# Three PSUM banks for the attention's logits instead of two, one for the output projection instead of two

## The chip, the cores and the metric

The kernel runs on one core of one Trainium2 chip. The metric is the device time of one execution in microseconds (us). TensorE is called PE in the profile, its weight loads PEld; VectorE is DVE, ScalarE is ACT, GpSimd is POOL, SyncE (which here only issues DMAs) is SP. PSUM is the small memory that PE writes its results to; it has 8 banks, each 128 partitions by 512 float32.

## What is computed

One layer of a decoder trunk, 1024 tokens by 1024 channels, float32. The reference, cut to what matters here:

```python
h = rms_norm(x, norm_mix_pre)
q, k_c, v_c, k_s, v_s, k_w, v_w, gate, u, v = split(h @ w_in)
# 8 heads, 3 branches each, on blocks of 128 queries:
p_c = softmax(q @ kc.T + bias)          # compressed keys (63)
p_s = softmax(q @ k_s.T + bias)         # selected blocks (here all of the causal ones)
p_w = softmax(q @ k_w.T + bias)         # window of 512
nsa = g0 * p_c @ vc + g1 * p_s @ v_s + g2 * p_w @ v_w
gm  = gelu(u) * (w_s @ layer_norm(gelu(v)) + b_s)
h1  = x + rms_norm(concat(nsa, gm) @ w_out, norm_mix_post)
out = h1 + rms_norm(swiglu(rms_norm(h1, norm_ffn_pre)), norm_ffn_post)
```

## The kernel before

The work is cut into tiles of 128 tokens, and runs in this order.

1. **Input side (0 to some 265 us).** `norm_in` normalizes and transposes the tokens; `vu_half` multiplies them by the v and u columns of `w_in` (into banks `ps_a` and `ps_w`); `spatial`, `proj_t`, `compress_in`, `compress_out` and `v_proj` make the gating part (kept in DRAM as `gm_scr`), the queries (in DRAM as `q_scr`), keys (`kt`) and values (`vt`). Every product that must be exact to float32 is made of three matmuls of split operands (`mm3`, L183 to L185).
2. **Attention (some 244 to 592 us).** The loop at L640 takes the tiles 7, 6, ... 0, and in each tile four pairs of heads. For a head, `logits` (L671) makes one chunk of logits of up to 512 columns in a bank `ps_a`, by two matmuls (L674, L675); DVE takes it out of the bank with the bias added, or plain (`biased` L679, `plain` L683), into the row buffer `L`. ACT makes the exponentials (L722), POOL multiplies by the gate over the sum (L733), PE transposes (L745, banks `ps_t`), ACT and DVE split the result (`ph`, `pl`, L167 and L173), and PE multiplies by the values (L752, L754, bank `ps_p`). `otmp`, `os`, `mixh`, `mixl` (L756 to L761) are the pair's result.
3. **Output projection.** While the attention of a tile runs, `output_proj` (L596) multiplies the result of the tile before by `w_out`: two halves `nh` of 512 columns, 24 matmuls each, of which 12 read the gating part `gmh` and 12 the attention's `mixh`, `mixl`. Each half has a bank `ps_w`; ACT reads the bank twice (L614 square, L615 copy). Then come the norm (L617 to L622), a store of `h1`, and `pre_ffn` (L626): square, scale (L628, L630), eight transposes (L634, banks `ps_t`), a scaling on DVE (L636) and a store to `h2_scr`.
4. **FFN (from some 597 us).** First `plain_pass` (L881) over tokens 512 to 1023 in banks `ps_a`, `ps_w`, `ps_p`, from operands `b12`, `b22` (profile name `b_b12t`, `b_b`) and `plain_op`; then these pools are closed, and the eight banks become the ring `fb`, in which all the rest is done. The second `plain_pass` needs the tokens 0 to 511, so the `h2` of tile 0.

The lines that matter for the change:

```python
109  TAGS = {"a": 2, "t": 3, "p": 1, "w": 2}
118  def bank(tag):
119      return psp[tag][1].tile([P, 512], F32, name="ps_" + tag)
121  for tag in ("a", "w", "t", "p"):
122      psp[tag] = pool("ps_" + tag, TAGS[tag], space=PSUM)
340  ps = turn("proj", "aaaw")
484  ps = turn("vproj", "wpt")
591  PVB, OPB, OB = "p", "w", 1
607  for nh in range(2):
608      ps = turn("opj", OPB)
610      for k in range(KD):
613          mm3(ps, sh, sl, wo[kk][0][:, cs], wo[kk][1][:, cs], k == 0, k == KD - 1)
614      nc.scalar.activation(h1[:, cs], ps, AF.Square, accum_out=s2[:, nh:nh + 1])
615      nc.scalar.copy(h1[:, cs], ps)
672  ps = bank("a")
674  nc.tensor.matmul(ps[:, :w], qt[:, 0, hh, :], kt_[g][:, c0:c0 + w], start=True, stop=False)
675  nc.tensor.matmul(ps[:, :w], qt[:, 1, hh, :], kt_[g][:, c0:c0 + w], start=False, stop=True)
776  return turn("plain", "awap")
```

`turn` (L113) takes the pools of a string in turn: L340 is in `proj_t`, L484 in `v_proj`, L776 in the first `plain_pass`; L607 to L615 are `output_proj`, L672 to L675 `logits`. A tile of a pool with n buffers waits until the tile n places before it in the same pool has been read. The order of the instructions on each engine is not the order of the code: the framework puts them in order when the kernel is built, by a plan of when each could run (`schedule_with_timeline_sim=True`, L1210) and by the priorities in the code (`tc.high_priority(...)`, L648 to L735). On the chip every engine then runs its own list strictly in order, and waits at the first instruction that is not ready.

Of the kernel before, what the change touches and what calls it, by code (L numbers as in the profile page):

```python
# [70 lines left out]
def trunk_kernel(ctx, tc, x, rel_bias, norm_mix_pre, norm_mix_post, norm_ffn_pre, norm_ffn_post, w_in,  # L71
# [7 lines left out]
    def pool(name, bufs, side=None, **kw):  # L79
        if side is not None:  # L80
            kw["side"] = side
        g = tc.tile_pool(name=name, bufs=bufs, reuse_waits="tile", **kw)
        return g, g.__enter__()
# [22 lines left out]
    psp = {}  # L106
    dram = ctx.enter_context(tc.tile_pool(name="dram", bufs=1, space=DRAM))

    TAGS = {"a": 2, "t": 3, "p": 1, "w": 2}

    turns = {}

# [8 lines left out]
    for tag in ("a", "w", "t", "p"):  # L121
        psp[tag] = pool("ps_" + tag, TAGS[tag], space=PSUM)
    for tag in ("whi", "wlo"):
# [1090 lines left out]
```

## Time and profile before

| | |
|---|---|
| median of 3 runs | 1249.96 us (1245.37 to 1250.56) |
| the profiled execution, its own time | 1250.03 us |
| its span, first to last instruction | 1248.3 us |
| PE busy | 1201.0 us, 96% of the span |
| DVE busy | 922.4 us, 74% |
| ACT busy | 568.4 us, 46% |
| POOL busy | 383.4 us, 31% |
| mean granted TensorE clock | 0.993 |

Busy time of PE is the union of its matmuls from start to modelled end; as matmuls overlap, a busy PE can still have started fewer of them than it could. The count of instructions in a stretch (the x in the windows) tells more. "Idle before" is the time that an engine stood still just ahead of an instruction, and the name behind the arrow is what ended it. An "until" list of a line gives the same for all instructions of that line, with total time and count.

### The profile page before, as it was taken

What the parts mean: (1) busy time and instruction counts of PE and PEld (TensorE: products, weight loads), DVE (VectorE), ACT (ScalarE), POOL (GpSimd) and SP (SyncE); (2) the same over time, 40 slices, a digit from 0 to 9 for tenths busy, and PEclk for the clock granted to TensorE, in tenths of its full rate; (3) what the DMA queues carried; (4) which work ended last, traced back from release to release, by engine and by line L of the source; (5) the groups of instructions that cost most, each with busy time, mean ns of one, the idle gap of its engine ahead of it and who ended that gap; (6) DMA issues with size and microseconds to landing.
All of it is one profiled execution on the core that took longest, in us unless ns stands there. A gap on an engine that the chain in (4) does not pass through costs nothing.

```text
span 1248.3 us, 18189 instructions
## 1 busy us (share of the span) xinstructions
PE 1201.0 (96%) x6074; PEld 1008.8 (81%) x6074; DVE 922.4 (74%) x2071; ACT 568.4 (46%) x1254; POOL 383.4 (31%) x454
## 2 busy tenths in 40 slices
PE   6999999889999999998899999999999999999997
PEld 5888878878888888887687888888888888888886
DVE  5646237668898988986599887876787647588996
ACT  4423022246777878886544332333332324444452
POOL 3315113155445446562051222201222101132341
PEclk9999999999999999999999999999999999999999
DMA  7212453321021121424414233223233189332235
GB/s 259 86 66 87 135 178 117 106 93 48 10 81 43 48 81 48 140 77 137 145 65 152 100 120 127 94 89 108 91 127 124 53 287 359 122 110 85 94 119 202
DMA packets 106229, 143.86 MB, mean 115 GB/s; under 512 B 8120, under 2 KB 64792, under 8 KB 106136
## 3 DMA queue, kind: packets, MB, share of 16 engines
q1 hardware_dynamic: 99552, 133.43, 32.4%
q0 software_dynamic: 2304, 4.20, 1.2%
q10 hardware_dynamic: 4280, 5.08, 1.2%
q8 instruction: 48, 0.79, 0.3%
q14 instruction: 45, 0.37, 0.1%
HBM read 103.60 MB, written 40.71 MB: 116 GB/s over the span
## 4 chain that ended last, share of the span: by engine, by line
PE 84%; DVE 9%; ACT 2%; issue 2%; DMA 1%; POOL 1%; SPq 0%; DVEq 0%; POOLq 0%; ACTq 0%
PE fb L185 16%; PE fb L183 15%; PE fb L184 15%; PE ps_w L183 4%; PE ps_w L184 4%; PE ps_w L185 4%; PE ps_a L183 4%; PE ps_a L184 3%; PE ps_a L185 3%; PE ps_t L745 3%; PE ps_p L754 2%; PE ps_p L752 2%; PE ps_a L674 2%; PE ps_a L675 2%; DVE pl L173 1%
## 5 line engine op out<-in xcount | busy, mean ns | idle before, releaser
L967 DVE TENSOR_TENSOR cc<-fb,cc 128x512 f32<-128x512 f32 x140 | 94.2, 685 | 55.9 <-PE fb L185 55.1
L722 ACT ACTIVATE L<-L,mm 128x64 f32<-128x64 f32 (+8 forms) x192 | 116.2, 608 | 37.0 <-DVE mm L679 36.2
L733 POOL TENSOR_SCALAR L<-L,wts 128x64 f32<-128x64 f32 (+8 forms) x192 | 108.4, 588 | 74.1 <-DVE wts L728 53.4
L848 POOL TENSOR_TENSOR cc<-sil 128x512 f32<-128x512 f32 x22 | 35.2, 1601 | 287.4 <-issue 226.3
L173 DVE TENSOR_TENSOR pl<-ps_t,ph 128x512 fp32r<-128x512 f32 (+1 forms) x160 | 101.6, 643 | 11.2 <-ACT ph L167 10.6
L167 ACT CAST op<-s 128x512 fp32r<-128x512 f32 x80 | 49.4, 620 | 121.5 <-PE fb L185 106.7
L184 PE MATMUL fb<-wdo,hido 128*128 128x512 f32 x264 | 102.7, 389 | 0.0
L183 PE MATMUL fb<-wdo,hido 128*128 128x512 f32 x264 | 101.9, 389 | 0.0
L185 PE MATMUL fb<-wdo,hido 128*128 128x512 f32 x264 | 100.4, 389 | 0.0
L184 PE MATMUL fb<-b_b,op 128*128 128x512 f32 x256 | 99.6, 389 | 0.0
L183 PE MATMUL fb<-b_b,op 128*128 128x512 f32 x256 | 99.3, 389 | 0.0
L185 PE MATMUL fb<-b_b,op 128*128 128x512 f32 x256 | 99.3, 389 | 0.0
L167 ACT CAST ph<-ps_t 128x512 fp32r<-128x512 f32 (+1 forms) x160 | 84.4, 555 | 25.6 <-PE ps_t L745 23.1
L745 PE MATMUL ps_t<-ident,L 128*128 128x128 f32 x592 | 88.6, 274 | 1.5 <-DVE pl L173 0.9
L674 PE MATMUL ps_a<-kt,qt 128*128 128x448 f32 (+4 forms) x208 | 74.7, 363 | 7.3 <-DVE L L683 2.8
L173 DVE TENSOR_TENSOR hido<-hidr,hido 128x512 fp32r<-128x512 f32 x77 | 60.8, 801 | 27.3 <-ACT hido L167 27.2
L167 ACT CAST hido<-hidr 128x512 fp32r<-128x512 f32 x77 | 47.4, 619 | 66.3 <-PE fb L185 22.8
L1046 POOL TENSOR_TENSOR tt<-wdr 128x512 f32<-128x512 f32 x22 | 36.1, 1644 | 134.5 <-DVE wdo L173 80.1
L754 PE MATMUL ps_p<-pl,vt 128*128 128x256 f32 x264 | 74.3, 303 | 3.1 <-DVE pl L173 3.0
L745 PEld LDWEIGHTS ps_t<-ident,L 128*128 128x128 f32 x592 | 68.9, 141 | 9.5 <-POOL L L733 1.8
L167 ACT CAST op<-wraw 128x512 fp32r<-128x512 f32 x60 | 37.1, 622 | 84.3 <-PE fb L185 75.6
L173 DVE TENSOR_TENSOR op<-s,op 128x512 fp32r<-128x512 f32 x80 | 63.9, 804 | 14.6 <-ACT op L167 13.8
(359 smaller groups left out, 3468.2 us busy)
## 6 DMA issues: line engine op xcount, KB each, us to landing
wraw<-in_w_gate_up_dram SPq DMA_DIRECT2D x40, 512.0 KB, 3.6
hidr<-hid_scr SPq DMA_DIRECT2D x77, 256.0 KB, 2.7
hid_scr<-sil SPq DMA_DIRECT2D x44, 256.0 KB, 2.0
wdr<-in_w_down_dram SPq DMA_DIRECT2D x44, 256.0 KB, 5.5
hid_scr<-cc SPq DMA_DIRECT2D x33, 256.0 KB, 2.0
xt<-in_x_dram SPq DMA_DIRECT2D x16, 512.0 KB, 3.6
raw<-in_w_in_dram SPq DMA_DIRECT2D x16, 512.0 KB, 4.3
gm_scr<-gmt SPq DMA_DIRECT2D x16, 256.0 KB, 2.6
```

The lines of the kernel that those rows point to most:

```text
L167: nc.scalar.copy(hi, src)
L173: e.tensor_tensor(lo, src, fl(hi), op=ALU.subtract)
L183: nc.tensor.matmul(ps, sh, mh, start=first, stop=False)
L184: nc.tensor.matmul(ps, sh, ml, start=False, stop=False)
L185: nc.tensor.matmul(ps, sl, mh, start=False, stop=last)
L674: nc.tensor.matmul(ps[:, :w], qt[:, 0, hh, :], kt_[g][:, c0:c0 + w], start=True, stop=False)
L722: nc.scalar.activation(L[:, c0:c1], L[:, c0:c1], AF.Exp, bias=mm[:, col:col + 1], scale=-1.0, accum_out=sums[:, hh, br:br + 1])
L733: nc.gpsimd.tensor_scalar(pts[hh][:, c0:c1], pts[hh][:, c0:c1], wts[:, hh, br:br + 1], 1.0, op0=ALU.mult, op1=ALU.mult)
L745: nc.tensor.transpose(ps[:, (bi * 2 + hh) * P:(bi * 2 + hh + 1) * P], pts[hh][:, c0:c0 + P], ident)
L754: nc.tensor.matmul(pv[:, :256], v, pl[:, bi * 256:(bi + 1) * 256], start=False, stop=last)
L967: nc.vector.tensor_tensor(dst, ps, y_, op=ALU.add)
L1046: eng.tensor_tensor(dst, x_, y_, op=op)
```

## The change

```diff
-    TAGS = {"a": 2, "t": 3, "p": 1, "w": 2}
+    TAGS = {"a": 3, "t": 3, "p": 1, "w": 1}
```

The pool of `ps_a` gets a third bank, and that of `ps_w` keeps one; the sum stays eight. Nothing else is edited. No instruction is added or removed, but since the plan sees other waits, the order on the engines changes in many places. Three of them follow. The names with numbers are the program's tiles; a number is the same tile in both versions.

PE, early in the attention, around the chunk of logits `ps_a_2879` of tile 7. Before:

```order
L754 MATMUL ps_p_2563<-pl_2648,vt_1425 128x256
L674 MATMUL ps_a_2865<-kt1_1419,qt_2483 128x256
L675 MATMUL ps_a_2865<-kt1_1419,qt_2483 128x256
L674 MATMUL ps_a_2874<-kt1_1419,qt_2483 128x448
L675 MATMUL ps_a_2874<-kt1_1419,qt_2483 128x448
L674 MATMUL ps_a_2879<-kt1_1419,qt_2483 128x384
L675 MATMUL ps_a_2879<-kt1_1419,qt_2483 128x384
L674 MATMUL ps_a_2883<-kt1_1419,qt_2483 128x256
L675 MATMUL ps_a_2883<-kt1_1419,qt_2483 128x256
L745 MATMUL ps_t_2779<-ident_123,L_2675 128x128
```

Now:

```order
L745 MATMUL ps_t_2616<-ident_123,L_2526 128x128
L674 MATMUL ps_a_2879<-kt1_1419,qt_2483 128x384
L675 MATMUL ps_a_2879<-kt1_1419,qt_2483 128x384
L674 MATMUL ps_a_2883<-kt1_1419,qt_2483 128x256
L675 MATMUL ps_a_2883<-kt1_1419,qt_2483 128x256
L754 MATMUL ps_p_2563<-pl_2596,vt_1425 128x256
L752 MATMUL ps_p_2563<-ph_2595,vt_1425 128x256
```

The same chunk stands 53 rows earlier in PE's list (row 1394 before, 1341 now), ahead of value products (`ps_p_2563`) that it used to follow. Over most of the attention 5 to 11 more of the 208 chunks have been issued after about the same number of PE's matmuls, and 14 to 32 fewer of the output projection's 384; at the end of the attention both are level again.

PE, the change from the output projection of tile 1 (second half: `ps_w_6795`) to that of tile 0 (first half: `ps_w_7076`). Before:

```order
L754 MATMUL ps_p_6878<-pl_6885,vt_1425 128x256
L752 MATMUL ps_p_6878<-ph_6895,vt_1425 128x256
L754 MATMUL ps_p_6878<-pl_6896,vt_1425 128x256
L183 MATMUL ps_w_7076<-whi_2055,gmh_7069 128x512
L184 MATMUL ps_w_7076<-wlo_2056,gmh_7069 128x512
```

Now:

```order
L752 MATMUL ps_p_6947<-ph_6964,vt_1425 128x256
L754 MATMUL ps_p_6947<-pl_6965,vt_1425 128x256
L185 MATMUL ps_w_6795<-whi_2670,mixl_6236 128x512
L183 MATMUL ps_w_7076<-whi_2055,gmh_7069 128x512
L184 MATMUL ps_w_7076<-wlo_2056,gmh_7069 128x512
```

`ps_w_6795` and `ps_w_7076` are now one and the same bank, and the last matmul of the one stands right ahead of the first of the other. Before, the two halves of a tile were open at the same time and taken in turn; now the second half begins when the first is done.

PE, behind the last value products of the attention (`ps_p_7039`, tile 0). Before:

```order
L754 MATMUL ps_p_7039<-pl_7057,vt_1425 128x256
L183 MATMUL ps_w_7076<-whi_2670,mixh_6684 128x512
L184 MATMUL ps_w_7076<-wlo_2671,mixh_6684 128x512
L183 MATMUL ps_w_7103<-whi_2670,mixh_6684 128x512
L184 MATMUL ps_w_7103<-wlo_2671,mixh_6684 128x512
L185 MATMUL ps_w_7076<-whi_2670,mixl_6685 128x512
L185 MATMUL ps_w_7103<-whi_2670,mixl_6685 128x512
L183 MATMUL ps_a_7310<-b_b12t3_7261,plain_op_7264 128x512
```

Now:

```order
L754 MATMUL ps_p_7039<-pl_7057,vt_1425 128x256
L183 MATMUL ps_w_7076<-whi_2670,mixh_6684 128x512
L184 MATMUL ps_w_7076<-wlo_2671,mixh_6684 128x512
L185 MATMUL ps_w_7076<-whi_2670,mixl_6685 128x512
L183 MATMUL ps_a_7310<-b_b12t3_7261,plain_op_7264 128x512
L184 MATMUL ps_a_7310<-b_b12t3_7261,plain_op_7264 128x512
L183 MATMUL ps_w_7103<-whi_2055,gmh_7069 128x512
L184 MATMUL ps_w_7103<-wlo_2056,gmh_7069 128x512
```

The second half of tile 0 (`ps_w_7103`, 24 matmuls) used to be nearly done here; now it begins here, behind two matmuls of the FFN's first pass.

## Rows read from the trace of the kernel before

**Rows 1.** The page: busy time by engine, and the chain that ended last.
```profile
PE 1201.0 (96%) x6074; PEld 1008.8 (81%) x6074; DVE 922.4 (74%) x2071; ACT 568.4 (46%) x1254; POOL 383.4 (31%) x454
PE 84%; DVE 9%; ACT 2%; issue 2%; DMA 1%; POOL 1%; SPq 0%; DVEq 0%; POOLq 0%; ACTq 0%
```

**Rows 2.** Windows: stretch and length, busy (and count) by engine, clock, DMA share, GB/s.
```profile
100.00:200.00 100.00, 100.00 (x480) 83.08 (x479) 49.76 (x82) 17.93 (x35) 30.58 (x25) 1.00 0.41 128
200.00:300.00 100.00, 91.49 (x560) 79.71 (x558) 67.39 (x208) 43.42 (x94) 38.64 (x47) 0.97 0.33 103
300.00:400.00 100.00, 97.05 (x631) 85.03 (x630) 86.84 (x329) 73.45 (x178) 44.30 (x70) 1.00 0.15 43
400.00:500.00 100.00, 96.02 (x639) 84.99 (x637) 87.55 (x348) 78.57 (x207) 50.04 (x85) 1.00 0.18 55
560.00:620.00 60.00, 52.71 (x268) 43.45 (x267) 38.21 (x108) 36.06 (x89) 11.19 (x25) 0.94 0.43 138
700.00:1248.00 548.00, 540.13 (x2383) 447.05 (x2382) 410.66 (x586) 197.91 (x353) 115.07 (x78) 1.00 0.40 134
```

**Rows 3.** Line 674, first matmul of a logits chunk: what ended its idle time.
```profile
  PE ps_a L675: 6.7, 11
  DVE mm L679: 4.2, 12
  DVE L L683: 3.8, 11
```

**Rows 4.** Line 679, DVE taking logits out: what ended its idle time.
```profile
  PE ps_a L675: 24.6, 29
```

**Rows 5.** Timeline of PE, tile 1's projection to tile 0's (start, length, engine, line).
```profile
576.28 0.72 PE L185 MATMUL ps_w<-whi,mixl 128*128 128x512 f32 x2
579.12 0.50 PE L183 MATMUL ps_w<-whi,gmh 128*128 128x512 f32 x1 [1.19 <-ACT h L615]
```

**Rows 6.** Timeline of ACT, the same stretch.
```profile
577.04 0.61 ACT L614 ACTIVATE h<-ps_w 128x512 f32<-128x512 f32 x1
577.63 0.60 ACT L614 ACTIVATE h<-ps_w 128x512 f32<-128x512 f32 x1
578.45 0.62 ACT L615 COPY h<-ps_w 128x512 f32<-128x512 f32 x1
```

**Rows 7.** Timeline of all engines, from that projection to tile 1's transposes.
```profile
584.47 0.39 PE L185 MATMUL ps_w<-whi,gmh 128*128 128x512 f32 x1
584.70 0.28 PE L752 MATMUL ps_p<-ph,vch 128*128 128x256 f32 x1
584.76 1.15 ACT L630 ACTIVATE xt<-h,rstd 128x1024 f32<-128x1024 f32 x1 [0.85 <-POOL rstd L179]
585.41 0.40 PE L183 MATMUL ps_w<-whi,gmh 128*128 128x512 f32 x1
588.16 1.04 PE L634 MATMUL ps_t<-ident,xt 128*128 128x128 f32 x8
589.04 0.60 PE L745 MATMUL ps_t<-ident,L 128*128 128x128 f32 x4
591.35 0.38 PE L754 MATMUL ps_p<-pl,vch 128*128 128x256 f32 x1
```

**Rows 8.** Timeline of all engines, end of the attention to the FFN's first matmul.
```profile
592.75 0.37 ACT L756 COPY otmp<-ps_p 64x256 f32<-64x256 f32 x1 [0.56 <-PE ps_p L754]
593.02 2.18 ACT L167 CAST b_b12t<-b_r1t 128x512 fp32r<-128x512 f32 x4
594.65 0.50 PE L183 MATMUL ps_w<-whi,mixh 128*128 128x512 f32 x1 [1.99 <-DVE mixh L169]
595.11 2.18 ACT L167 CAST b_b<-b_r1t 128x512 fp32r<-128x512 f32 x4
597.18 0.62 ACT L167 CAST plain_op<-plain_raw 128x512 fp32r<-128x512 f32 x1
597.86 0.50 PE L183 MATMUL ps_a<-b_b12t,plain_op 128*128 128x512 f32 x1 [1.55 <-ACT plain_op L167]
```

**Rows 9.** Timeline of all engines, tile 0's transposes to the FFN's second half.
```profile
616.59 1.03 PE L634 MATMUL ps_t<-ident,xt 128*128 128x128 f32 x8
617.22 1.29 DVE L636 TENSOR_TENSOR h2s<-ps_t,gffn 128x512 f32<-128x512 f32 x2 [1.72 <-PE ps_t L634]
624.01 2.38 ACT L167 CAST b_b<-raw 128x512 fp32r<-128x512 f32 x4 [5.52 <-DMA raw<-h_scr]
```

**Rows 10.** DMA issues of `gmh`: size of one, median us from issue to landing.
```profile
gmh<-gm_scr POOLq DMA_DIRECT2D x16, 256.0 KB, 3.7
```

## The prediction

> **What bounds the kernel now.** I read the page first: PE is busy 96% of the span, and 84% of the chain that ended last is PE [rows 1]. So the time is PE's work plus what PE stands still, and the change has no other way to pay than through PE's waits. The windows by stage tell where those are [rows 2]. From 100 to 200 us PE is busy all the time; from 700 us on it starts 2383 matmuls in 548 us, nearly all of 512 columns, which is one every 0.23 us. Nothing can be gained there. From 200 to 620 us PE is not full, and beside it DVE is busy 87% to 88% and ACT 73% to 79% of the attention's middle: three engines that hand work to each other, with little room in any.
>
> Then I looked at what the two pools of the change make PE wait for. PE's first matmul of a logits chunk (L674) found its engine idle until DVE had taken out an earlier chunk: 4.2 us in 12 cases and 3.8 us in 11, and 6.7 us more in 11 cases are put down to PE's own matmul before [rows 3]. In turn DVE, taking logits out at L679, waited 24.6 us in 29 cases for PE [rows 4]. That is the picture of two engines that share two banks: each waits for the other by turns. For `ps_w` the trace shows one clear wait: ahead of tile 0's projection PE stood 1.19 us for ACT's reading of a bank [rows 5].
>
> **The change part by part.** The profiled execution took 1250.03 us, 0.07 above the median of the runs shown, so I sum against 1250.03.
>
> *Input side: 0.* `vu_half` uses `ps_w` once in every 48 matmuls; 24 of `ps_a` (5.4 us at 0.23) lie between, and cover one ACT reading of about 0.6 us, the length of L614 [rows 6]. `proj_t` takes `w` every fourth time, `v_proj` every third. If a cover failed, it would cost one such reading, so I bound this part by 1 us either way.
>
> *Logits: -8.0.* With a third bank, L674 waits for the chunk three places back. The waits that DVE's L679 and L683 ended are 4.2 + 3.8 = 8.0 us [rows 3]. I take these as gone, since they are what a bank more removes directly. The other end is that the 6.7 us go too: -14.7. The upper end is 0: DVE is 87% busy [rows 2] and takes out no more logits per us because PE makes them earlier. The order agrees that chunks move forward, but a chunk that is issued earlier can also wait at an earlier place.
>
> *Handovers of the single `ps_w`: +3.8.* First the price. After the last matmul of a half (modelled end 576.28 + 0.72 = 577.00 [rows 5]) ACT starts L614 at 577.04, the next ACT instruction of that kind follows 0.59 later, and L615 takes 0.62 [rows 6]. So the bank is free about 1.25 us after that end; as a matmul would otherwise start some 0.2 us ahead of the end of the one before, an open handover costs about 1.5 us. Of 15 handovers within the output projections, 11 now have 10 to 36 other matmuls between. The shortest of these (six transposes, two logits, two value products at about 0.12 us, as six value products take 585.41 - 584.70 = 0.71 [rows 7]) covers 1.2 us, the rest 2 to 4 us; I cost them at 0, with 0.5 each, so 5.5, as the other end. Four, at the end of the attention, are bare: tile 2 to tile 1 with nothing between (1.5), tile 1's halves with six value products between (1.5 - 0.7 = 0.8), tile 1 to tile 0 with nothing between (1.5), and tile 0's halves with two matmuls between. In the last, ACT's list has eight casts of `b12` and `b22`, a cast of `plain_op`, L614, another `plain_op`, L615. The casts end where they ended before, at about 597.7 [rows 8]; 0.6 + 0.55 + 0.62 later is 599.5. PE starts its two matmuls at 597.86 and is through at 598.3: 1.2. Sum 5.0, less the 1.19 that one of them cost before: +3.8.
>
> *Transposes of `pre_ffn`: +3.0.* With the halves one after the other, the second ends later. Between its end and the transposes (L634) stood 82 matmuls for tile 2 and 50 for tile 1; now 21 in both, which is 4.7 us. The chain that must pass in that time, from 577.00 to the end of L630 at 584.76 + 1.15 = 585.91, is 8.9 us [rows 5, 7]; one L614 and one L615 of it, 1.2 us, now fall earlier. Remain 7.7, less 4.7, less the 1.5 of the handover in it: 1.5 for each tile. Everything on PE is queued behind these transposes. Ends: 0, and 5.4 if ACT and DVE have other work between.
>
> *Last pair: +2.1.* From tile 0's transposes (L745, 589.04) to the value products (591.35) PE had six matmuls of the projection to do; now none, 6 x 0.23 = 1.4. And three matmuls fewer stand ahead of the first FFN matmul, whose start ACT sets [rows 8]: 0.7.
>
> *Given back: -2.9.* From 560 to 620 us PE idled 60 - 52.7 = 7.3 us [rows 2]. 1.19, 1.99 and 1.55 of it [rows 5, 8] I have kept; the other 2.6 are waits for softmax steps, which get time while PE stands elsewhere: I take -2.0. Tile 0's transposes stand four matmuls earlier, and from them to the cast that opens the second half (616.59 to 624.01 [rows 9]) the chain is fixed: -0.9.
>
> *Queues: 0.* On SP the four `plain_raw` loads now go ahead of three `wraw` loads; both stay behind tile 1's `h2` stores, and `wraw` is first needed after the whole first pass. On POOL `gmh` can be reloaded only when the second half has read it; 1.2 us for two issues and 3.7 to landing [rows 10] are about 4.9, and in tiles 1 and 0 some 3.5 us of matmuls and the 1.5 us of the handover lie over it.
>
> The end of the attention comes to 3.8 + 3.0 + 2.1 - 2.9 = +6.0, with ends 0 and 9. The sum: 1250.03 - 8.0 + 6.0 = **1248.0 us**.
>
> **The rivals.** *Faster.* All 14.7 us of L674's waits go, since DVE, which stood 24.6 us waiting for logits [rows 4], is fed earlier, and half of the +6.0 is covered by work that the plan has ready: 1250.0 - 14.7 + 3.0 = 1238.3. Against it: DVE's 87%.
>
> *Slower.* ACT runs in order and is up to 79% busy in the attention [rows 2]. If L614 and L615 stand in its list behind exponentials and casts that come late, the bank is returned late in the 11 covered handovers too. It decides from the point where the return takes longer than the 1.2 to 4 us of other matmuls. At 1 us each: 1250.0 - 8.0 + 6.0 + 11 = 1259. For it: before, two banks were open at once and the order of ACT hardly mattered; against it: in all but one the plan has put 17 matmuls or more between. The Trainium skill ("Perfetto Trace Analysis", Optimizing Tensor Performance, Matmuls) asks that independent groups of matmuls rotate through different PSUM banks, so that the evacuation of one overlaps the matmuls of the next. It speaks against the half of the change that leaves `ps_w` one bank: by it every one of the 15 handovers would pay, an estimate of 15 x 1.5 = 22.5 us, and the time would be 1250.0 - 8.0 + 22.5 = 1264.5. The trace agrees that such a wait exists [rows 5], but matmuls of other groups can fill it.
>
> *No gain from logits.* DVE is the bound of the attention, and only the end's cost remains: 1250.0 + 6.0 = 1256.0.
>
> **How the numbers follow.** What a measurement of this kernel can tell from no change is about 0.5%, 6.2 us: 1243.8 to 1256.2. My forecast (some 1243 to 1252) has 0.38, the faster rival 0.27, the slower 0.22, no gain from logits 0.13. Faster: 0.27 and 0.05 from the forecast's edge, 0.32. Slower: 0.22 and 0.04 of the last case, 0.26. Within: 0.42. The range takes in the faster rival's 1238.3 and the slower's 1259 with about a us beyond each: 1237 to 1260; the likeliest case's own is 1243 to 1252.
>
> **What would show it.** Right: at L674 the idle time ended by L679 and L683 falls from 8.0 to under 3 us; between 560 and 620 us PE starts fewer matmuls than 268; ahead of `ps_w` matmuls ACT's L615 ends 4 to 6 us of idle time in all, and L630 ends some 3 us ahead of L634; the windows to 200 us and from 700 us on stay as they are, shifted. Wrong: L674's waits stay, only at other places (then the gain is not there); `ps_w` waits are spread over 300 to 560 us (the slower rival); or the end of the attention is as quick as before (then my +6.0 is not there, and the time is near 1242).

## The result and the profile after

The changed kernel takes 1257.43 us in the median of four runs (1256.22 to 1258.79), the kernel before 1249.35 (1245.37 to 1250.56). The ratio is 1.0071, with a 95% interval of 1.0045 to 1.0096: slower by 0.7%, more than the 0.5% that a measurement can tell from no change. The forecast was 1248.0, 2 us quicker than before; the measured change goes the other way. The time is inside the range, on the side that had a chance of 0.26.

The page's busy times and the chain of the changed kernel, which answer to [rows 1]:

```profile
PE 1201.1 (96%) x6074; PEld 1009.8 (80%) x6074; DVE 916.1 (73%) x2071; ACT 568.1 (45%) x1254; POOL 372.7 (30%) x454
PE 79%; DVE 10%; ACT 3%; DMA 3%; issue 2%; POOL 2%; SPq 0%; POOLq 0%; DVEq 0%; ACTq 0%
```

PE is busy as long as before to 0.1 us. Five points of the chain have passed from PE to engines and transfers that PE waits for. The windows of the changed kernel, with the columns of [rows 2], say in which stages:

```profile
300.00:400.00 100.00, 98.26 (x662) 87.83 (x661) 91.33 (x358) 76.81 (x189) 51.46 (x77) 1.00 0.13 38
400.00:500.00 100.00, 96.97 (x658) 86.89 (x656) 89.82 (x350) 79.52 (x212) 50.36 (x89) 1.00 0.26 79
560.00:620.00 60.00, 48.78 (x231) 38.42 (x230) 34.80 (x99) 34.89 (x84) 8.38 (x19) 0.90 0.41 131
```

The attention's middle is quicker: 662 and 658 matmuls started in the two windows, 631 and 639 in [rows 2]. Its end is slower: 231 in place of 268. Three more windows of the kernel before, with the same columns:

```profile
40.00:50.00 10.00, 10.00 (x54) 8.32 (x53) 7.87 (x14) 6.50 (x14) 2.65 (x4) 1.00 0.40 130
260.00:500.00 240.00, 229.08 (x1488) 200.66 (x1486) 205.22 (x786) 175.50 (x437) 122.13 (x186) 0.99 0.18 56
500.00:560.00 60.00, 58.42 (x372) 50.52 (x371) 53.00 (x226) 50.44 (x166) 36.09 (x75) 1.00 0.34 104
```

The same three of the changed kernel:

```profile
40.00:50.00 10.00, 6.64 (x22) 5.34 (x22) 8.67 (x18) 5.32 (x11) 4.79 (x6) 0.66 0.19 60
260.00:500.00 240.00, 233.68 (x1580) 209.48 (x1579) 217.67 (x842) 184.02 (x466) 130.75 (x200) 1.00 0.21 64
500.00:560.00 60.00, 52.57 (x317) 43.91 (x316) 43.06 (x186) 43.72 (x147) 31.20 (x69) 0.99 0.25 81
```

Two of the three losses stand where the forecast had none to speak of: 40 to 50 us (22 matmuls for 54, at a granted clock of 0.66), and 500 to 560 us (317 for 372).

To add the stages up I use **PE's lost time**: the length of a stretch, less for each matmul that starts in it the usual step to the next start for its shape (the lower quartile in the kernel before, 0.227 us for one of 512 columns). It counts idle time and slow matmuls alike and is worked out from all of PE's rows. In us, with the median of the timed runs behind:

```
                        0-60  60-260  260-500  500-560  560-640    time
before                  15.0    14.4     29.9      6.0     15.0   1249.4
the change              21.6    13.6     19.5     13.5     19.5   1257.4
change minus before     +6.6    -0.8    -10.4     +7.5     +4.5
e1 u products on two    17.5    14.0     22.1     11.9     21.3   1253.6
e2 last tiles on two    19.5    14.3     19.8      5.4     12.5   1243.1
e3 both                 15.5    13.8     21.1      4.8     11.1   1238.8
e4 one ps_w, two ps_a   22.0    14.9     31.2     16.1     22.3   1278.2
e5 tiles 2, 1 on two    21.4    13.5     19.5      5.1     16.5   1245.6
e6 tile 0 on two        20.9    13.5     20.2     14.1     16.8   1254.3
e7 two gmh              20.2    14.0     22.4     11.9     22.7   1259.9
e8 three ps_a, two ps_t 17.5    10.5     35.9     11.1     13.7   1260.4
e9 before, one u bank   22.0    13.0     30.2      6.2     12.8   1257.3
e10 copy first          19.5    13.5     25.4     14.4     22.6   1266.5
e11 both, all tiles     16.2    13.9     23.6      4.8     14.0   1239.4
e12 both, tiles 3 to 0  16.2    13.0     19.1      5.8     10.0   1235.9
```

The five differences sum to +7.4; the two spans differ by 1255.5 - 1248.3 = 7.2. Behind 640 us nothing has changed (4.9 us lost in either). So the change is a gain of about 10 us and two losses, of 7 and 12 us. "The middle" below is 260 to 500 us, "the end" 500 to 640 us. The table is from one profiled execution of each kernel, and an edit in one stage shifts the plan in the others too: a stage that an edit doesn't touch differs by up to 2.6 us (the middle of e1 beside that of the change). I read nothing from less than 3 us in one stage.

### The profile page after: what moved, and what is told of

It reads as the page before. It is cut to its first block, busy times and chain, and to the rows that moved or that the text cites. A ratio compares the mean times of both kernels' runs of the same rounds, so it can differ in the third digit from the quotient of the medians.

```text
span 1255.5 us, 18190 instructions
## 1 busy us (share of the span) xinstructions
PE 1201.1 (96%) x6074; PEld 1009.8 (80%) x6074; DVE 916.1 (73%) x2071; ACT 568.1 (45%) x1254; POOL 372.7 (30%) x454
## 4 chain that ended last, share of the span: by engine, by line
PE 79%; DVE 10%; ACT 3%; DMA 3%; issue 2%; POOL 2%; SPq 0%; POOLq 0%; DVEq 0%; ACTq 0%
PE fb L185 15%; PE fb L184 15%; PE fb L183 15%; PE ps_w L183 4%; PE ps_w L184 4%; PE ps_w L185 4%; PE ps_a L183 3%; PE ps_a L185 3%; PE ps_a L184 3%; PE ps_t L745 3%; DVE pl L173 2%; PE ps_p L752 2%; PE ps_p L754 2%; PE ps_a L674 2%; PE ps_a L675 1%
## 5 line engine op out<-in xcount | busy, mean ns | idle before, releaser
L733 POOL TENSOR_SCALAR L<-L,wts 128x64 f32<-128x64 f32 (+8 forms) x192 | 108.8, 588 | 84.9 <-DVE wts L728 52.1
L722 ACT ACTIVATE L<-L,mm 128x64 f32<-128x64 f32 (+8 forms) x192 | 116.0, 606 | 28.7 <-DVE mm L679 25.4
L173 DVE TENSOR_TENSOR pl<-ps_t,ph 128x512 fp32r<-128x512 f32 (+1 forms) x160 | 100.8, 643 | 12.2 <-ACT ph L167 11.8
L745 PE MATMUL ps_t<-ident,L 128*128 128x128 f32 x592 | 90.2, 275 | 7.3 <-DVE pl L173 3.5
L745 PEld LDWEIGHTS ps_t<-ident,L 128*128 128x128 f32 x592 | 68.5, 140 | 17.8 <-DVE pl L173 4.8
L674 PE MATMUL ps_a<-kt,qt 128*128 128x448 f32 (+4 forms) x208 | 71.1, 347 | 3.3 <-DVE mm L679 2.0
```

What stands on the lines that cost most here:

```text
L173: e.tensor_tensor(lo, src, fl(hi), op=ALU.subtract)
L722: nc.scalar.activation(L[:, c0:c1], L[:, c0:c1], AF.Exp, bias=mm[:, col:col + 1], scale=-1.0, accum_out=sums[:, hh, br:br + 1])
L733: nc.gpsimd.tensor_scalar(pts[hh][:, c0:c1], pts[hh][:, c0:c1], wts[:, hh, br:br + 1], 1.0, op0=ALU.mult, op1=ALU.mult)
L745: nc.tensor.transpose(ps[:, (bi * 2 + hh) * P:(bi * 2 + hh + 1) * P], pts[hh][:, c0:c0 + P], ident)
```

## The experiments

My theory after reading the trace: a bank for a long accumulation is a place in which filler, work that PE can do while nothing else is ready, can stand open. With two `ps_w`, two products of 24 matmuls are open at once, and the plan lays their matmuls into the gaps of the work beside them. With one, the second can't be begun until the first is complete and ACT has read it; the gaps stay empty. The rival was the prediction's own account: each change of owner costs the wait for ACT, about 1.5 us where nothing covers it. "by turns" below is the kernel's own `turn`.

**e1, e2, e3: a second bank at the start, at the end, and both.** In the changed kernel `ps_p` is first written at 200 us, so it lies idle while `vu_half` runs, and I took it that the logits need few banks when the last tiles' projections come.

```diff
e1, vu_half, u product:
-            ps = bank("w")
+            ps = turn("vu", "wp")
e2, output_proj:
-            ps = turn("opj", OPB)
+            ps = turn("opj", "wa") if i <= 2 else bank("w")
e3: both edits
```

> The changed kernel with its u products of the input side (vu_half) taken by turns from ps_w and ps_p, a bank that is idle there; everything else as in the change. Theory S (the one ps_w costs about 6 us in the first 50 us, since the u product of tile 1 can't stand open beside that of tile 0 while tiles 2 and 3 are still being normalized): the window 40 to 50 us returns from 22 matmul records at a granted clock of 0.66 to about 50 records at 1.00, and the time falls from 1257.4 to about 1251 (1249 to 1253). Rival N (the hole of 40 to 44 us comes from the norm and its transposes, which a second u bank does not hurry): the window stays as in the change and the time within 1 us of 1257.4.

Measured: 1253.58 us (1249.82 to 1257.32, 11 runs), ratio to before 1.003 (1.0017 to 1.0044), 0.6 above the range expected. The window of e1 is back to what it was before the change:

```profile
40.00:50.00 10.00, 10.00 (x54) 8.36 (x53) 7.64 (x13) 4.91 (x10) 2.96 (x4) 1.00 0.24 78
```

3.9 us of the expected 6 came back. In the profiled execution, which took 1256.51, the first 40 us have 113 matmuls at a clock of 0.96, where the changed kernel has 124 at 1.00; by the lost time that is 2.0 us. Whether it is in every execution of a spread of 7.5 us, one profile can't say.

> The changed kernel with the output projections of tiles 2, 1 and 0 alone taken by turns from ps_w and ps_a, at a time when the logits need few banks; tiles 7 to 3 keep one ps_w. Theory E (the last 130 us of the attention lose about 12 us against before, about two thirds of them since the last tiles' projection halves wait for ACT L615 to give the single ps_w back and since less work stands ready beside them): the waits of ps_w on L615 at 584 and 601 us go, and the time falls from 1257.4 to about 1250 (1246 to 1253). Rival (the end is paced by the attention's own chain, L759 to the splits to the matmuls, and by the reload of gmh, whatever banks the halves have): the time stays within 2 us of 1257.4, with other waits in the same holes.

Measured: 1243.08 us (1242.23 to 1245.17), ratio 0.9955 (0.9944 to 0.9967): 14.4 us below the change, below the range expected. The last two stages of e2:

```profile
500.00:560.00 60.00, 58.25 (x359) 50.33 (x358) 44.44 (x185) 45.40 (x148) 32.36 (x71) 1.00 0.30 90
560.00:640.00 80.00, 72.58 (x341) 58.69 (x342) 57.69 (x131) 45.44 (x103) 19.12 (x21) 0.96 0.38 124
```

PE is busy 58.25 of the 60 us to 560, for 52.57 in the change, and 72.58 of the next 80. Three halves on a borrowed `ps_a` (tiles 2, 1 and 0 have one each) take back the whole loss of the end and a little more: 17.9 us of lost time from 500 to 640 us, beside 33.0 in the change and 21.0 before.

> Both edits together: u products by turns from ps_w and ps_p, output projections of tiles 2, 1 and 0 by turns from ps_w and ps_a. If both losses are of the single ps_w and the gain of the third ps_a in the middle (about 13 us from 250 to 500 us) stands by itself: 1257.4 - 6 - 7 = about 1244 (1239 to 1248), below the kernel before. If only the start is of the bank: about 1251; if neither: 1257.

Measured: 1238.83 us (1236.54 to 1240.08), ratio 0.9917 (0.9904 to 0.993), just under the range expected. The gains add: 14.4 for the end, and 4.3 more for the start, close to e1's 3.9. With both losses mended the kernel is 10.7 us quicker than before (1249.5 - 1238.8). That this is so near the 10.4 of the middle is chance: by the table, from a profiled execution of 1236.54 us, the middle gains 8.8 us (21.1 for 29.9) and the end 5.1 (15.9 for 21.0), so that halves on a borrowed `ps_a` do better there than two `ps_w` did.

**e4: one `ps_w` without the third `ps_a`.**

```diff
-    TAGS = {"a": 3, "t": 3, "p": 1, "w": 1}
+    TAGS = {"a": 2, "t": 3, "p": 1, "w": 1}
```

> Half of the change alone: one ps_w as in the change, but two ps_a as before, so that one PSUM bank stands unused. Theory (the third ps_a gains about 13 us in the middle, the lost ps_w costs about 6 at the start and about 12 at the end): 1249.4 + 18 = about 1267 (1262 to 1271). Rival (the third ps_a itself brings the losses, as it pulls the logits ahead and leaves less beside the last projections): about 1255 (1252 to 1258), with the end as in the kernel before but for four handovers of ps_w.

Measured: 1278.19 us, ratio 1.0236 (1.0221 to 1.025), 28.7 above before and 7 above the range expected. The rival falls: the losses are there without the third `ps_a`, and the end's are larger. The window of e4's middle shows 1492 matmuls, as many as the 1488 before, for 1580 with three `ps_a`:

```profile
260.00:500.00 240.00, 227.02 (x1492) 198.33 (x1492) 200.69 (x775) 172.65 (x430) 117.89 (x175) 1.00 0.18 52
```

So the middle's gain belongs to the third `ps_a`. At the end e4 loses 16.1 + 22.3 us, 5.4 more than the change, a part that I had not added. My reading, which no run shows by itself, is that a third chunk of logits is filler there too.

**e5, e6: which tiles of the end.**

```diff
e5:
+            ps = turn("opj", "wa") if i in (2, 1) else bank("w")
e6:
+            ps = turn("opj", "wa") if i == 0 else bank("w")
```

> The changed kernel with the output projections of tiles 2 and 1 alone by turns from ps_w and ps_a; those of tiles 7 to 3 and of tile 0 keep the single ps_w. Filler theory (two halves open at once let the matmuls of both, above all the 12 + 12 on gmh that need no fresh mixh, lie in the gaps of the attention; with one bank half 1 can't begin before half 0 is complete and copied out): most of what tiles 2, 1 and 0 together gave back (14.4 us) is here, 9 to 13 us, so about 1246 (1244 to 1248.5). Handover theory (each half waits only for ACT L614 and L615 to give the bank back, 1.5 us at each of the three handovers of these tiles, plus 3 us for the transposes behind them): at most 7 us, so 1250 or above.

> The changed kernel with the output projection of tile 0 alone by turns from ps_w and ps_a. It has hardly any other work of the attention beside it. Filler theory: little to fill, so the handover alone counts, 1 to 3 us, so about 1255.5 (1254 to 1256.5); together with the tiles 2 and 1 of the run beside it this should add up to the 14.4 us of the three tiles. Rival (the end is one chain, and the last pair sets it): 5 us or more, 1252 or below.

Measured: e5 1245.63 us (11.8 below the change; ratio to before 0.9977, 0.9968 to 0.9986), e6 1254.26 (3.2 below; 1.0048, 1.003 to 1.0066). Both are in the range of the filler theory. 11.8 + 3.2 = 15.0, beside 14.4 for the three tiles at once; e6's interval overlaps the change's (1.0045 to 1.0096), so that the 3.2 by itself is not settled. Four fifths are with tiles 2 and 1, where the prediction's handovers and transposes came to 6.8, and with the upper end of the transposes to 9.2. With one bank, half 0 of tile 2 stands open for the last of `mixh`, and half 1 can't lie beside it. What is missing is seen in the windows, of `ps_w` matmuls alone, of the kernel before (time, busy and count, clock, DMA share, GB/s):

```profile
530.00:535.00 5.00, 0.66 (x3) 1.00 0.44 106
535.00:540.00 5.00, 1.06 (x4) 1.00 0.74 238
540.00:545.00 5.00, 1.72 (x6) 1.00 0.09 26
```

and of the changed kernel:

```profile
530.00:535.00 5.00, 0.00 (x0) 1.00 0.55 148
535.00:540.00 5.00, 0.00 (x0) 1.00 0.31 91
540.00:545.00 5.00, 1.03 (x3) 1.00 0.00 0
```

Before, 12 matmuls of the projection start in these 15 us, among the attention's (one lies across 535 us and counts in two windows); now 3 do. ACT's timeline tells the same: before, the first readings (L614) of tile 2's halves start at 550.05 and 551.02, so both halves were open to the end; in the change they start at 544.89 and 554.63, one after the other:

```profile
544.89 0.60 ACT L614 ACTIVATE h<-ps_w 128x512 f32<-128x512 f32 x1
554.63 0.60 ACT L614 ACTIVATE h<-ps_w 128x512 f32<-128x512 f32 x1 [0.27 <-PE ps_w L185]
```

**e7: two buffers of `gmh`.**

```diff
-        gmh = at["late"].tile([P, 2, 4, P], F32R, name="gmh", bufs=1)
+        gmh = at["late"].tile([P, 2, 4, P], F32R, name="gmh", bufs=2)
```

> The changed kernel with two buffers of gmh instead of one, so that the reload of a tile's gated half need not wait until the halves of the tile before have read the first. The reload ended a wait of 2.08 us of the projection at 556.7 us in the changed kernel, where none had been forecast. If that wait is a cost by itself: about 1255.4 (-1.5 to -2.5). If the reload only stands for the late end of half 1 and the next wait takes its place: within 1 us of 1257.4.

Measured: 1259.85 us, ratio 1.0091 (1.0074 to 1.0109), 2.4 above the change and outside both expectations; its interval overlaps the change's, so that a loss isn't settled either. PE's timeline of the changed kernel at the end has these rows, with the idle time before each and what ended it:

```profile
528.17 0.50 PE L183 MATMUL ps_w<-whi,mixh 128*128 128x512 f32 x1 [1.46 <-ACT mixh L167]
556.68 0.47 PE L183 MATMUL ps_w<-whi,gmh 128*128 128x512 f32 x1 [2.08 <-DMA gmh<-gm_scr]
572.02 0.89 PE L745 MATMUL ps_t<-ident,L 128*128 128x128 f32 x4 [1.89 <-POOL L L733]
584.32 0.50 PE L183 MATMUL ps_w<-whi,gmh 128*128 128x512 f32 x1 [1.61 <-ACT h L615]
590.62 1.09 PE L634 MATMUL ps_t<-ident,xt 128*128 128x128 f32 x8 [1.23 <-ACT xt L630]
596.34 0.79 PE L183 MATMUL ps_w<-whi,mixh 128*128 128x512 f32 x1 [1.93 <-DVE mixh L169]
```

In e7 the wait for the reload is gone, and one of the same length stands at the transposes of `pre_ffn` that come next:

```profile
565.24 1.51 PE L634 MATMUL ps_t<-ident,xt 128*128 128x128 f32 x8 [1.97 <-ACT xt L630]
```

In the change these transposes, at 563.38, had no wait. The end as a whole loses 34.6 us, for 33.0 in the change. The reload named in the change's row ended the wait, but nothing was gained without it, as it would be if PE had nothing else to run there.

**e8: the third `ps_a` from the transposes.**

```diff
+    TAGS = {"a": 3, "t": 2, "p": 1, "w": 2}
```

> Three ps_a as in the change, but the bank is taken from the transposes (three ps_t become two) and ps_w keeps its two. If the transposes of the attention can do with two banks, the gain of the third ps_a in the middle (about 10 us) comes without the losses of the single ps_w: 1249.5 - 10 = about 1239 (1236 to 1243). If the third ps_t is needed by L745 and its split, as before the change L745 stood 592 times, every second one then waits for ACT or DVE to empty a bank: slower than before, 1255 to 1290.

Measured: 1260.41 us, ratio 1.01 (1.0073 to 1.0128). The middle loses 35.9 us, more than before the change. Who waited for the attention's transposes (L745, total us and cases) in e8:

```profile
  ACT ph L167: 50.1, 61
```

and in the changed kernel:

```profile
  ACT ph L167: 14.9, 16
```

With two `ps_t` the casts behind L745 stand 50.1 us waiting for transposes that come late. That `ps_t` can spare the bank is refuted. (In the kernel before, with three `ps_t`, it was 23.1 us.)

**e9: the kernel before with one bank for u products.**

```diff
-            ps = bank("w")
+            ps = bank("p")
```

> The kernel BEFORE (two ps_a, two ps_w) with the u products of the input side on ps_p alone, so that only one of them can be open at a time; the attention is untouched. If the loss of the first 60 us is that of the second open u product and of nothing else: 40 to 50 us falls from 54 matmul records to about 20 to 30 at a granted clock below 1.00, and the time rises by about 4 to 7 us, to about 1254 (1252 to 1256). If the start of the changed kernel lost its time by another move of the plan: within 1 us of 1249.

Measured: 1257.34 us (1254.76 to 1259.6), ratio 1.006 (1.0042 to 1.0078), 7.9 us above before: the start's loss alone, in a kernel whose attention is untouched, though a little more than the 4 to 7 us expected. Its window:

```profile
40.00:50.00 10.00, 5.97 (x18) 4.51 (x17) 8.58 (x15) 5.80 (x13) 3.98 (x4) 0.68 0.20 55
```

18 matmuls at 0.68, as in the change. The place is plain in PE's timeline of the changed kernel:

```profile
40.44 0.63 PE L240 MATMUL ps_t<-ident,xt 128*128 128x128 f32 x4 [0.42 <-DVE ms L177]
44.01 1.08 PE L240 MATMUL ps_t<-ident,xt 128*128 128x128 f32 x4 [2.94 <-issue]
44.74 0.78 PE L183 MATMUL ps_w<-whi,xTh 128*128 128x512 f32 x1
45.31 0.63 PE L184 MATMUL ps_w<-wlo,xTh 128*128 128x512 f32 x1
45.74 0.63 PE L185 MATMUL ps_w<-whi,xTl 128*128 128x512 f32 x1
```

and of the kernel before:

```profile
41.10 0.48 PE L184 MATMUL ps_w<-wlo,xTh 128*128 128x512 f32 x1
42.78 0.39 PE L185 MATMUL ps_w<-whi,xTl 128*128 128x512 f32 x1
43.31 0.59 ACT L317 ACTIVATE gu<-ps_w 128x512 f32<-128x512 f32 x1
44.74 0.62 ACT L317 ACTIVATE gu<-ps_w 128x512 f32<-128x512 f32 x1
```

Before, the second u product ran from 41 to 43 us while the next tile was still being normalized, and ACT read both at 43.31 and 44.74. In the change the bank is read at 42.95, and the next u matmul starts at 44.74.

**e10: the bank given back sooner.**

```diff
-            nc.scalar.activation(h1[:, cs], ps, AF.Square, accum_out=s2[:, nh:nh + 1])
             nc.scalar.copy(h1[:, cs], ps)
+            jq = at["late"].tile([P, 512], F32, name="jq", bufs=1)
+            nc.scalar.activation(jq, h1[:, cs], AF.Square, accum_out=s2[:, nh:nh + 1])
```

> The changed kernel with its single ps_w given back sooner: ACT copies the half to h1 first, and the Square for the norm then reads h1, not the bank; so the bank waits for one ACT operation of 0.6 us instead of two with a read of the accumulator between (0.60 + 0.20 + 0.59 us), at all 16 halves. Handover theory (the end's 12 us are waits for ACT to give ps_w back): a gain of 3 us or more, 1254 or below. Filler theory (what is missing is a second open accumulation, whatever the handover takes): within 2 us of 1257.4.

Measured: 1266.54 us, ratio 1.0129 (1.0098 to 1.016), 9 above the change; neither theory had that. Who waited for the copy (L614 here) in e10:

```profile
  PEld ps_w L183: 1.7, 3
  PE ps_w L183: 0.3, 1
```

and for L615, which gives the bank back, in the changed kernel:

```profile
  PEld ps_w L183: 6.0, 4
  PE ps_w L183: 2.2, 2
```

The wait for the bank all but went, and no time was gained: the end loses 37.0 us, for 33.0 in the change. Instead PE's transposes of `pre_ffn` waited for L631 (L630 in the change, where PE waited 1.5 us in 2 cases):

```profile
  PE ps_t L635: 6.7, 3
```

That is 5.2 us more. And PE was slower. The windows of e10's end have a granted clock of 0.91 and 0.89, where the change has 0.99 and 0.93:

```profile
500.00:560.00 60.00, 53.67 (x320) 46.22 (x320) 41.69 (x186) 43.38 (x146) 29.74 (x63) 0.91 0.22 62
560.00:640.00 80.00, 67.56 (x313) 53.49 (x312) 43.04 (x122) 39.60 (x94) 10.52 (x26) 0.89 0.44 142
```

Behind 640 us e10 loses 9.2 us, for 4.9. Its four runs go by their mean clock: 1269.44 us at 0.978, 1268.77 at 0.979, 1264.30 at 0.983 and 1260.98 at 0.987, the clock of the change's 1257.21. So more than half of the 9 us goes with the clock, and e10 is no clean test of the handover. What speaks against the handover theory is the change's own list above. Of the idle time of PE's matmuls, L615 ended 2.2 us, in the two handovers at 584.32 and 601.66; with the 2.08 at 556.68, where the reload came last, that is 4.3 of the 12 us. (The 6.0 us are of weight loads, which stood at the same three handovers but for 0.3 us.)

**e11, e12: how far the turn-taking should reach.** Both have e3's edit of the u products.

```diff
e11:
+            ps = turn("opj", "wa")
e12:
+            ps = turn("opj", "wa") if i <= 3 else bank("w")
```

> The u products by turns from ps_w and ps_p, and the output projections of all tiles by turns from ps_w and ps_a, not of tiles 2, 1 and 0 alone. In tiles 7 to 3 the attention has enough other work, and each half there holds a ps_a from the logits while it stands open. If the third ps_a is what the middle gains by, part of that is given back: 1240 to 1246, slower than 1238.8. If the early tiles too lack a second open half: 1234 to 1238.

> The same with the output projections of tiles 3, 2, 1 and 0 by turns from ps_w and ps_a. At tile 3's projection the logits of tile 2 still fill PE: 1237 to 1241, within 2 us of the version for tiles 2, 1 and 0 (1238.8). If the gap grows gradually and tile 3 is already short of filler: 1234 to 1237.

Measured: e11 1239.44 us (1238.29 to 1242.14; ratio 0.992, 0.9905 to 0.9936), e12 1235.89 (1233.76 to 1238.86; ratio 0.9897, 0.988 to 0.9914). e11's median is half a us below the range I gave and 0.6 above e3, and its interval overlaps e3's: lending a `ps_a` to the early tiles too shows neither gain nor loss. That its middle loses 23.6 us, for 21.1 in e3, is within what two profiles differ by. e12 is the quickest of all, in the range I gave for a tile 3 that is short of filler. Its ratio to before and e3's overlap at the edge, so that tile 3 gains 3 us over e3 is likely, not settled. Both e3 and e12 beat the two kernels of the case.

## Why the prediction was wrong

The forecast summed -8.0 for the logits and +6.0 for the end of the attention; by the stages the change brought -10.4 and +12.0, and +6.6 at the start, where the forecast had 0. Two steps failed: the input side's, and the end's.

**The input side: 0, bounded by 1 us; measured +6.6.** This step failed outright. It read the loop of `vu_half`, found "24 of `ps_a`" between two uses of `ps_w`, and asked whether they cover one reading by ACT. But the plan doesn't run the loop in its order: while tiles 2 and 3 were being normalized, both u products were open and were PE's only work. What had to be asked is what PE runs while nothing else is ready, and into which banks; the timeline of 38 to 45 us would have told. e9 gives the loss alone, e1 takes most of it back.

**Logits: -8.0, with -14.7 as the other end; measured -10.4.** Right in kind, and wrong in which waits go; that the size is near is luck. I took L679's and L683's 8.0 us as gone and left L675's 6.7. What L679 and L683 ended of L674's idle time in the changed kernel, beside [rows 3] (L675 is not in the list any more):

```profile
  DVE mm L679: 4.0, 5
  DVE L L683: 0.8, 1
```

L675's 6.7 us are gone and 4.8 of the 8.0 stay, where I had asked for under 3. But I read such a list as the idle time of PE's matmuls, and it counts that of the weight loads (PEld) with it. The rows of L674 by engine, before:

```profile
L674 PE MATMUL ps_a<-kt,qt 128*128 128x448 f32 (+4 forms) x208 | 74.7, 363 | 7.3 <-DVE L L683 2.8
L674 PEld LDWEIGHTS ps_a<-kt,qt 128*128 128x128 f32 x208 | 39.6, 191 | 17.6 <-PE ps_a L675 6.7 <-DVE mm L679 3.1 <-issue 2.7
```

and in the change:

```profile
L674 PE MATMUL ps_a<-kt,qt 128*128 128x448 f32 (+4 forms) x208 | 71.1, 347 | 3.3 <-DVE mm L679 2.0
```

The 6.7 us are all of weight loads, and of the matmuls' own idle time there were 7.3 us in all, of which 4.0 went. So neither -8.0 nor -14.7 was a sum of time that PE's matmuls stood idle. By the windows from 260 to 500 us PE's idle time in all fell from 10.9 us (240 - 229.08) to 6.3, which is 4.6 of the 10.4; the rest are matmuls that started later than the usual step while the one before still ran, a part of them at the lower clock (0.99 for 1.00). That the gain is the logits' chunks' holds: by the lost time, the steps that end at L674 and L675 go from 15.3 us to 6.9. DVE's wait for L675 at L679, 24.6 us in [rows 4], is now

```profile
  PE ps_a L675: 10.9, 13
```

and DVE is busy 91% and 90% in the two windows, above the 87% to 88% that I had taken as an argument against the faster rival.

**The end of the attention: +6.0, with ends 0 and 9; measured 7.5 + 4.5 = +12.0.** The price of a bare handover was about right (1.5; the one at 584.32 waited 1.61), and so was that of tile 1's transposes (1.5; the row at 590.62 has 1.23), though tile 2's had no wait: L630 ended 1.5 us in all, for the 3 forecast. At the bare handovers PE stood 4.3 us in all; L615 ended 2.2 of it, where I had asked for 4 to 6. What failed is the step "the shortest of these covers 1.2 us, the rest 2 to 4 us; I cost them at 0": a handover with other matmuls in it was taken as free, because only the wait was priced. By the windows of `ps_w` under e5, half 1's matmuls had themselves been PE's work while it would have waited for others, as it now does for L733 and `mixh` in the rows under e7. e5 puts 11.8 us on tiles 2 and 1, whose steps came to 6.8. The last pair and its handover, 2.1 + 1.2, are near e6's 3.2, which the spread of its runs (1250.83 to 1257.34) may have brought about. Where I did count filler (82 matmuls to 21 ahead of L634) I did so for one wait, not for all those in the stretch.

**Queues: 0.** The `gmh` reload of tile 1 did end a wait of 2.08 us, so there it was not covered as I had said. In e7 that wait is gone and no time with it, since the next takes its place.

**The rivals.** The slower one, 1259, is near the time for a reason that the change's list of L615 refutes: of PE's matmuls only those of two bare handovers waited for it, none of the 11 covered ones. ACT did come late in one of them (tile 2's half 0 ended at 542.43, L614 started at 544.89), but the 22 other matmuls lay over it. The faster one's 1238.3 is near e3's 1238.8, a kernel that keeps two halves open at the start and the end; the change itself shows only the middle's part of it. No gain from logits, 1256.0, is near the time too, and the middle's 10.4 us refute it.

One `ps_w` without the third `ps_a` costs 28.7 us (e4), above the 22.5 that I had estimated from 15 handovers at 1.5. It isn't made of such waits: about 7 us are the start (22.0 for 15.0), and of the idle time of PE's matmuls ahead of `ps_w` L615 ended 2.0 us in e4, in 4 cases.

The Trainium skill ("Perfetto Trace Analysis", Optimizing Tensor Performance, Matmuls) asks that independent groups of matmuls rotate through different PSUM banks. The runs agree with the advice (e2, e5 and e3 follow it, and are quicker than the change); its reason, the evacuation of one group beside the matmuls of the next, is here the smaller part of the price.

## What to carry to other kernels

A PSUM bank is worth the waits that its chunks suffer and the filler that it holds open: before a bank is taken from a long accumulation, look what PE runs in the places where nothing else is ready, and whether two accumulations are open there at once. A pool need not own a bank for the whole kernel; halves that borrow an idle or little used bank for one stage (here `ps_p` at the start, `ps_a` for the last tiles) kept most of the middle's gain (8.8 of 10.4 us) and took back 18.6 (1257.4 to 1238.8). And a wait that a row names is a cost only if PE has something to run once it is gone (e7).

## What was not expected of the hardware

A hole on PE cost nearly twice its length at the start. From 40 to 50 us PE was idle 10 - 6.64 = 3.4 us, and the stretch lost 6.2. Behind the idle 2.94 us the 512-column matmuls from 44.74 start 0.57 and 0.43 us apart, and not 0.227, and the window's granted clock is 0.66: PE ran a part of it at the lower of its two levels, 1.2 GHz. The kernel before, with PE busy through the same 10 us, shows 1.00 there. e9 has the same hole: 4.0 us idle, a clock of 0.68, and 6.9 us lost. More idle time and a lower clock go together at the end of the attention too, where the changed kernel's clock from 560 to 620 us is 0.90 for 0.94 in [rows 2].
